# Activation slots and weight buffers at 2 KB boundaries of the on-chip memory

## Chip, cores and metric

The kernel runs on one core of a Trainium2 chip. The metric is device time in microseconds (us) of one execution; lower is better. The core has five engines with queues of their own: TensorE (PE in the profile; its weight loads are shown as PEld), VectorE (DVE), ScalarE (ACT), GpSimd (POOL) and SyncE (SP), which here issues the DMA transfers. Tiles lie in the on-chip memory (SBUF), which has 128 partitions; an address below is a byte offset within a partition and is the same in all 128.

## What is computed

Two small transformer-like blocks, one behind the other, on 256 tokens of width 1,024, all in 32-bit floats. Cut to the parts that make up the work:

```python
# first block, two layers
for l in range(DEPTH):
    h = rmsnorm(x, g_mix[l])
    # layer 0: conformer convolution of h @ w_in_a; layer 1: forgetting attention
    x = x + concat([mix, memory_attention(...)]) @ w_out[l]
    x = x + conv_ffn(rmsnorm(x, g_ffn[l]), w_up[l], w_dw_f[l], b_dw_f[l], w_down[l])
# second block: retention layer, a gated embedding, a sparse attention layer, a gated embedding
h = h + (silu(gate) * groupnorm(retention(q, k, v))) @ ret_w_out
h = h + sigmoid(rmsnorm(h) @ w_gate) * (p_i @ w_emb)
h = h + (silu(gate) * (g0 * o_compressed + g1 * o_selected + g2 * o_window)) @ nsa_w_out
```

Nearly all the arithmetic lies in products of a 1,024-wide or 2,816-wide activation with weights that are read once.

## The kernel before

Activations are kept transposed: a chunk is 128 features by 256 tokens, and a width of 1,024 makes eight chunks. Weights are one long stream of units, each 128 partitions by 1,024 floats (512 KB), in the order in which they are used.

To keep precision with the faster 32-bit matmul form, most operands are split in two, a rounded "hi" and a remainder "lo". One weight block times one chunk then is three matmuls (`mm3`, lines 543 to 546): hi by hi (544), hi by lo (545), lo by hi (546), where the first name is the weight block, which is loaded into the array (128 columns), and the second the activation half, which streams through it (256 columns). `proj` (line 557) walks the chunks of an activation, takes the next weight block with `wblk`, and calls `mm3`. In the first stage ("conv") unsplit weights are multiplied directly (line 562).

An activation chunk lies in a *slot*, a tile of 512 floats (2 KB per partition): its first KB is hi, its second lo. The class `Slots` (line 357) holds a list of free slots and hands out the one that has been free longest. 38 slots are allocated at line 399, and seven *late* ones in `phase("ffn0")` from a pool that opens there (line 433).

A weight unit arrives by a DMA of SyncE in a `raw` buffer (lines 476 and 477). ScalarE rounds it to `whi` (line 492), VectorE or GpSimd subtracts to give `wlo` (line 495), and TensorE reads eight blocks of 512 bytes per partition from each. There are four raw buffers (pool `wraw`) and six of each of the other two (pool `wspl`), 4 KB each. `LOOK` lets the splitting run some four units ahead of the multiplications.

Addresses: tiles are laid out in the order in which pools are opened and, within a pool, in the order in which tiles are allocated, each rounded up to 32 bytes. The pool `const` (line 392) comes first, then `wraw`, `wspl`, `fp`, `tiny`, and then the pools of the phases. The pool `const` begins at 16,512, behind a reserved area. In the kernel before, its first tiles are the 38 slots, then come `one`, `par`, `xall`, `cst`, `ones`, `mhalf`, `epsc`, `bgh` and the other small tiles, `onesT` (line 1089), `bgate` (line 1559) and `pcz0` last. By the layout of this kernel:

```
what                     first address   behind a 2 KB boundary (bytes)
slots 0 to 37            16512           128
par, xall                94368, 97920    160, 1664
raw, whi, wlo buffers    110400          1856   (4096 bytes each)
fp (working tiles)       175936          1856
late slots 38 to 44      198336          1728
```

The small tiles: `ones` holds ones for sums over partitions, `epsc` a constant added in a root, `onesT` the ones of a scan (line 1090 fills it), and `bg` the gates of the last attention (line 1560). The scheduler that builds the program does not keep the written order of independent instructions; it places them by a simulated time.

Of the kernel before, what the change touches and what calls it, by code (L numbers as in the profile page):

```python
# [18 lines left out]
F32 = mybir.dt.float32  # L19
# [5 lines left out]
P = 128  # L25
T = 256
# [361 lines left out]
def block_kernel(ctx, tc, A, out, WL, PL, CL, SL, stop=None, dbg=None):  # L388
# [3 lines left out]
    const = ctx.enter_context(tc.tile_pool(name="const", bufs=1))  # L392
# [3 lines left out]
    tiny = ctx.enter_context(tc.tile_pool(name="tiny", bufs=4))  # L396
    dram = ctx.enter_context(tc.tile_pool(name="dram", bufs=1, space=bass.MemoryType.DRAM))
    psum = ctx.enter_context(tc.tile_pool(name="psum", bufs=1, space=bass.MemoryType.PSUM))
    slots = Slots(const, NSLOTS - LATE)

    cnt = [0]
# [130 lines left out]
        return cst[:, o:o + n]  # L532

    ident = par[:, PL.off["ident"]:PL.off["ident"] + P]
    ones = const.tile([P, P], F32, name="ones")
    pool.memset(ones, 1.0)
    mhalf = const.tile([P, 2], F32, name="mhalf")
    pool.memset(mhalf, -0.5)
    epsc = const.tile([P, 2], F32, name="epsc")
    pool.memset(epsc, 1e-6)  # L540


# [532 lines left out]
    FR = 38  # L1075
# [10 lines left out]
    act.activation(za[0:FR, :], za[0:FR, :], AF.Exp, scale=-1.0)  # L1086
    act.activation(za[0:FR, :], za[0:FR, :], AF.Ln, bias=1.0)
    dve.scalar_tensor_tensor(zl[0:FR, :], z[0:FR, :], 0.0, za[0:FR, :], op0=OP.min, op1=OP.subtract)
    onesT = const.tile([FR, T], F32, name="onesT")
    pool.memset(onesT, 1.0)  # L1090
    cl = f1()
    dve.tensor_tensor_scan(cl[0:FR, :], onesT, zl[0:FR, :], 0.0, op0=OP.mult, op1=OP.add)
# [463 lines left out]
    pb = bank()  # L1556
    for tt in range(2):
        pe.transpose(pb[:, 64 * tt:64 * tt + 48], zb[0:48, P * tt:P * tt + P], ident[0:48, 0:48])
    bg = const.tile([P, 2, 48], F32, name="bgate")
    act.copy(bg, pb[:, 0:128].rearrange("p (t c) -> p t c", t=2)[:, :, 0:48])  # L1560

    SC128 = 128.0 ** -0.5
# [266 lines left out]
```

## Time and profile before

| | us |
|---|---|
| runs of the kernel before: lowest, median, highest | 1,216.21, 1,219.66, 1,224.07 |
| the profiled execution, whole | 1,224.89 |
| its span, first to last instruction | 1,223.1 |
| TensorE busy within the span | 1,177.8 |
| VectorE, ScalarE, GpSimd busy | 933.1, 720.3, 396.0 |

The mean granted TensorE clock of the profiled execution is 0.989. "Busy" of TensorE adds up the spans of pipelined matmul records that overlap, so it says when TensorE has work, not how fast it goes; the pace is read from start times. Lines are those of the kernel file, and a line of a helper such as `mm3` collects the work of all its callers. A tile is named without its buffer number, so the trace does not say which slot an instruction read; where the text does, it follows from the program's own list of instructions, which stand in the trace in the same order on TensorE.

### The profile page before, as it was taken

Reading aid. Unit: us, or ns where it says so; the run is one execution under the profiler, and the core shown is the slowest. Engines: PE = TensorE matmul, PEld = TensorE weight load, DVE = VectorE, ACT = ScalarE, POOL = GpSimd, SP = SyncE. Lnnn points to the kernel's source line nnn. Section 1 sums busy time; section 2 is a strip of 40 time slices with the busy share of each in tenths; the row PEclk is TensorE's granted clock in tenths of the full one; section 3 lists DMA queues with packets and bytes.
Section 4 is the critical chain, followed back from the end, with each engine's and each line's share of the span. In section 5 each row is a group of like instructions: output and inputs, shape, how many; then the busy total and the mean of one; then the engine's idle time right before and its main releaser. Section 6 shows DMA issues by size and latency. Waiting matters only on the chain.

```text
span 1223.1 us, 23147 instructions
## 1 busy us (share of the span) xinstructions
PE 1177.8 (96%) x8924; PEld 1128.9 (92%) x8924; DVE 933.1 (76%) x1610; ACT 720.3 (59%) x1336; POOL 396.0 (32%) x302
## 2 busy tenths in 40 slices
PE   7999999999999999899999999999999999999996
PEld 6888999999989999899999999999998899888996
DVE  1896799995568988998656876757896778979574
ACT  3855667665566766666554555445665756556545
POOL 3862412212413243222242222213444432222251
PEclk9999999999999999999999999999999999999998
DMA  9822545665544335555654655555566743332260
GB/s 352 294 96 66 172 159 190 204 206 184 182 137 138 122 129 173 174 188 193 203 183 155 199 169 176 189 169 184 163 199 233 249 139 104 121 104 96 87 207 35
DMA packets 59870, 205.60 MB, mean 168 GB/s; under 512 B 6640, under 2 KB 9072, under 8 KB 59760
## 3 DMA queue, kind: packets, MB, share of 16 engines
q1 hardware_dynamic: 59760, 204.12, 50.5%
q8 instruction: 70, 1.15, 0.4%
q14 instruction: 40, 0.33, 0.1%
HBM read 202.00 MB, written 2.10 MB: 167 GB/s over the span
## 4 chain that ended last, share of the span: by engine, by line
PE 79%; DVE 12%; ACT 4%; issue 3%; DMA 1%; POOL 0%; SPq 0%; DVEq 0%; ACTq 0%; POOLq 0%
PE acc L544 11%; PE acc L545 11%; PE acc L546 11%; PE s L544 5%; PE s L545 5%; PE s L546 5%; PE pt L544 4%; PE pt L545 4%; PE pt L546 4%; PE acc L562 4%; DVE wlo L495 3%; PE pt L562 2%; PE pt L665 2%; ACT whi L492 1%; DVE slot L595 1%
## 5 line engine op out<-in xcount | busy, mean ns | idle before, releaser
L492 ACT CAST whi<-raw 128x1024 fp32r<-128x1024 f32 x341 | 355.3, 1048 | 213.9 <-PE acc L545 90.1
L495 POOL TENSOR_TENSOR wlo<-raw,whi 128x1024 fp32r<-128x1024 f32 x94 | 231.7, 2465 | 535.5 <-ACT whi L492 428.3
L495 DVE TENSOR_TENSOR wlo<-raw,whi 128x1024 fp32r<-128x1024 f32 x247 | 322.8, 1309 | 102.9 <-ACT whi L492 99.6
L545 PE MATMUL acc<-slot,whi 128*128 128x256 f32 x1360 | 384.2, 283 | 0.5 <-DVE slot L595 0.2
L544 PE MATMUL acc<-slot,whi 128*128 128x256 f32 x1360 | 380.6, 283 | 4.0 <-ACT slot L592 1.8
L546 PE MATMUL acc<-slot,wlo 128*128 128x256 f32 x1360 | 382.7, 282 | 0.0
L544 PEld LDWEIGHTS acc<-slot,whi 128*128 128x128 f32 x1360 | 256.0, 189 | 6.1 <-ACT slot L592 2.0
L545 PEld LDWEIGHTS acc<-slot,whi 128*128 128x128 f32 x1360 | 257.8, 190 | 3.3 <-DVE slot L595 1.8
L546 PEld LDWEIGHTS acc<-slot,wlo 128*128 128x128 f32 x1360 | 257.8, 190 | 0.7
L544 PE MATMUL s<-slot,whi 128*128 128x256 f32 x508 | 144.1, 286 | 6.5 <-DVE ca L1009 4.0
L545 PE MATMUL s<-slot,whi 128*128 128x256 f32 x508 | 144.1, 284 | 1.5 <-DVE slot L581 1.5
L546 PE MATMUL s<-slot,wlo 128*128 128x256 f32 x508 | 143.2, 284 | 0.3 <-POOL wlo L495 0.3
L544 PE MATMUL pt<-slot,whi 128*128 128x256 f32 x468 | 131.3, 281 | 1.3 <-ACT slot L580 1.2
L545 PE MATMUL pt<-slot,whi 128*128 128x256 f32 x468 | 131.3, 281 | 0.0
L546 PE MATMUL pt<-slot,wlo 128*128 128x256 f32 x468 | 131.1, 280 | 0.0
L544 PEld LDWEIGHTS s<-slot,whi 128*128 128x128 f32 x508 | 96.7, 191 | 7.7 <-ACT whi L492 4.1
L545 PEld LDWEIGHTS s<-slot,whi 128*128 128x128 f32 x508 | 97.3, 192 | 1.7 <-DVE slot L581 1.7
L546 PEld LDWEIGHTS s<-slot,wlo 128*128 128x128 f32 x508 | 97.2, 192 | 0.5 <-POOL wlo L495 0.4
L610 POOL TENSOR_TENSOR sqa<-sqa,sq 128x256 f32<-128x256 f32 x54 | 56.2, 1044 | 118.4 <-ACT sq L614 117.4
L544 PEld LDWEIGHTS pt<-slot,whi 128*128 128x128 f32 x468 | 88.1, 188 | 1.8 <-ACT slot L580 1.4
L545 PEld LDWEIGHTS pt<-slot,whi 128*128 128x128 f32 x468 | 88.0, 188 | 0.0
L546 PEld LDWEIGHTS pt<-slot,wlo 128*128 128x128 f32 x468 | 87.9, 188 | 0.1
(381 smaller groups left out, 2102.3 us busy)
## 6 DMA issues: line engine op xcount, KB each, us to landing
raw<-ws SPq DMA_DIRECT2D x341, 512.0 KB, 3.5
wf<-ws SPq DMA_DIRECT2D x28, 512.0 KB, 8.2
xall<-xtok SPq DMA_DIRECT2D x2, 512.0 KB, 3.9
tok<-mtok SPq DMA_DIRECT2D x2, 512.0 KB, 10.2
mem<-memt SPq DMA_DIRECT2D x8, 128.0 KB, 6.1
emb<-em SPq DMA_DIRECT2D x4, 256.0 KB, 4.2
xall<-xt SPq DMA_DIRECT2D x4, 256.0 KB, 3.8
dm<-decay SPq DMA_DIRECT2D x4, 256.0 KB, 4.1
```

The lines of the kernel that those rows point to most:

```text
L492: act.copy(whi[i], raw[i])
L495: eng.tensor_tensor(wlo[i], raw[i], f32(whi[i]), op=OP.subtract)
L544: pe.matmul(ps, lhsT=ahi, rhs=bhi, start=start, stop=False)
L545: pe.matmul(ps, lhsT=ahi, rhs=blo, start=False, stop=False)
L546: pe.matmul(ps, lhsT=alo, rhs=bhi, start=False, stop=stop)
L562: pe.matmul(ps, lhsT=hi, rhs=s, start=start and k == 0, stop=stop and k == len(X) - 1)
L595: dve.scalar_tensor_tensor(s.lo, src, col, f32(s.hi), op0=OP.mult, op1=OP.subtract)
L610: pool.tensor_tensor(self.acc, self.acc, self.last, op=OP.add)
L665: pe.transpose(o, i, ident)
```

## The change

Three small tiles are allocated ahead of the slots, and one small tile is made wider. No operation is added, removed or moved in the text; `epsc` is filled in 56 columns where it was filled in two, and only its first column is read.

```diff
     psum = ctx.enter_context(tc.tile_pool(name="psum", bufs=1, space=bass.MemoryType.PSUM))
+
+    onesT = const.tile([38, T], F32, name="onesT")
+    ones = const.tile([P, P], F32, name="ones")
+    bg = const.tile([P, 2, 48], F32, name="bgate")
     slots = Slots(const, NSLOTS - LATE)
...
-    ones = const.tile([P, P], F32, name="ones")
     pool.memset(ones, 1.0)
...
-    epsc = const.tile([P, 2], F32, name="epsc")
+
+    epsc = const.tile([P, 56], F32, name="epsc")
     pool.memset(epsc, 1e-6)
...
-    onesT = const.tile([FR, T], F32, name="onesT")
     pool.memset(onesT, 1.0)
...
-    bg = const.tile([P, 2, 48], F32, name="bgate")
     act.copy(bg, pb[:, 0:128].rearrange("p (t c) -> p t c", t=2)[:, :, 0:48])
```

By the layout rule above, `onesT` (1,024 bytes), `ones` (512) and `bgate` (384) fill 16,512 to 18,432, which is 9 x 2,048. The slots begin there. The rest of the pool, with 216 bytes more for `epsc`, ends at 110,592, which is 54 x 2,048, and the raw, whi and wlo buffers begin there. Everything behind them moves by 192 bytes, so `fp` begins at 176,128 (0 behind a boundary), and the seven late slots at 198,528, which is 1,920 behind one.

## Rows read from the trace of the kernel before

**Rows 1.** The page: busy time (share of span), then the chain's shares by engine.
```profile
PE 1177.8 (96%) x8924; PEld 1128.9 (92%) x8924; DVE 933.1 (76%) x1610; ACT 720.3 (59%) x1336; POOL 396.0 (32%) x302
...
PE 79%; DVE 12%; ACT 4%; issue 3%; DMA 1%; POOL 0%; SPq 0%; DVEq 0%; ACTq 0%; POOLq 0%
```

**Rows 2.** Groups by line: busy us, mean ns of one, then idle before and releaser.
```profile
L545 PE MATMUL acc<-slot,whi 128*128 128x256 f32 x1360 | 384.2, 283 | 0.5 <-DVE slot L595 0.2
L546 PE MATMUL acc<-slot,wlo 128*128 128x256 f32 x1360 | 382.7, 282 | 0.0
L544 PE MATMUL acc<-slot,whi 128*128 128x256 f32 x1360 | 380.6, 283 | 4.0 <-ACT slot L592 1.8 <-DVE nq L1590 1.7 <-DVE slot L581 0.5
...
L544 PE MATMUL s<-slot,whi 128*128 128x256 f32 x508 | 144.1, 286 | 6.5 <-DVE ca L1009 4.0 <-ACT whi L492 2.6
...
L545 PE MATMUL pt<-slot,whi 128*128 128x256 f32 x468 | 131.3, 281 | 0.0
```

**Rows 3.** Timeline of TensorE, 1,506 intervals without a stall: start us, length us.
```profile
157.61 0.28 PE L546 MATMUL s<-slot,wlo 128*128 128x256 f32 x1
...
335.08 0.28 PE L546 MATMUL acc<-slot,wlo 128*128 128x256 f32 x1
```

**Rows 4.** The same view, another stretch, 50 intervals.
```profile
758.05 0.28 PE L545 MATMUL acc<-slot,whi 128*128 128x256 f32 x1
...
763.71 0.28 PE L544 MATMUL acc<-slot,whi 128*128 128x256 f32 x1
```

**Rows 5.** Windows: us, PE, PEld, DVE, ACT, POOL busy, clock, DMA share, GB/s.
```profile
157.60:335.10 177.50, 177.50 (x1509) 177.50 (x1508) 147.21 (x228) 111.09 (x182) 45.05 (x22) 1.00 0.58 188
...
646.40:806.10 159.70, 159.70 (x1141) 149.18 (x1140) 117.35 (x182) 81.52 (x119) 41.07 (x33) 1.00 0.53 174
```

**Rows 6.** Timeline of TensorE: the first and the last of 7,176 intervals between such matmuls.
```profile
95.99 0.28 PE L545 MATMUL acc<-slot,slot 128*128 128x256 f32 x1
...
1212.41 0.28 PE L546 MATMUL acc<-slot,wlo 128*128 128x256 f32 x1
```

**Rows 7.** Timeline of all engines, the first ten microseconds.
```profile
0.77 0.20 POOL L536 MEMSET ones<- 128x128 f32 x1
...
0.94 0.10 POOL L540 MEMSET epsc<- 128x2 f32 x1
...
5.58 0.30 POOL L1090 MEMSET onesT<- 38x256 f32 x1
...
6.19 0.56 POOL L688 TENSOR_TENSOR tn<-tn,mhalf 128x1 f32<-128x1 f32 x1
...
6.79 0.75 DVE L716 TENSOR_SCALAR xall<-xall,tn 128x1024 f32<-128x1024 f32 x1 [0.92 <-POOL tn L688]
...
7.60 0.69 PE L665 MATMUL acc<-par,xall 128*128 128x128 f32 x2 [7.60 <-DVE tn L687]
...
9.49 5.03 PE L562 MATMUL s<-sq,wf 128*128 128x256 f32 x11 [0.56 <-DMA wf<-ws]
```

**Rows 8.** Chain of waits at the start, in order of time: start us, us, what.
```profile
3.06 6.30 DMA wf<-ws
```

**Rows 9.** DMA issues: count, KB each, median us to landing.
```profile
raw<-ws SPq DMA_DIRECT2D x341, 512.0 KB, 3.5
...
xall<-xtok SPq DMA_DIRECT2D x2, 512.0 KB, 3.9
```

**Rows 10.** Timeline of TensorE: first and last of 702 matmuls that read late slots.
```profile
278.57 0.28 PE L544 MATMUL acc<-slot,whi 128*128 128x256 f32 x1
...
1178.25 0.28 PE L545 MATMUL acc<-slot,whi 128*128 128x256 f32 x1
```

**Rows 11.** The same view, slots by slots, 11 intervals.
```profile
351.28 0.28 PE L544 MATMUL s<-slot,slot 128*128 128x256 f32 x1
...
352.59 0.28 PE L546 MATMUL s<-slot,slot 128*128 128x256 f32 x1
```

**Rows 12.** Waits of TensorE, the longest: us in total, times, longest us.
```profile
PE acc L665 <- DVE tn L687: 7.6, 1, 7.6
```

## The prediction

> **What bounds the kernel now.** I read the page's busy shares and its chain of waits first. TensorE is busy 1,177.8 of 1,223.1 us, and 79% of the chain that ended last is its own work [rows 1]. No other engine comes near, so a change matters if it alters the pace at which matmuls follow each other, or adds a wait in front of them. The groups by line then say which matmuls: lines 544 to 546, the three products of one weight block with one activation chunk, stand 1,360, 508 and 468 times each, 3 x 2,336 = 7,008 matmuls [rows 2]. Their "mean ns of one" (281 to 286) is the length of a pipelined record, not the pace, so I took the pace from the timeline's start times. In a long stretch without a stall 1,506 intervals fill 335.08 - 157.61 = 177.47 us, 117.8 ns each [rows 3]. In another, 50 intervals fill 763.71 - 758.05 = 5.66 us, 113.2 ns each [rows 4]. Same shapes, same lines, and the granted clock is 1.00 around both [rows 5]: **there are two paces**. Sorting all 7,176 intervals between consecutive matmuls of this form (256 columns; first and last are in [rows 6]) into their 143 unbroken runs, 19 runs with 516 intervals keep the fast pace throughout, 113 runs with 6,354 intervals the slow one, 11 runs with 306 change on the way.
>
> The window from 157.6 to 335.1 us shows what else has room: TensorE busy for all 177.50 us, VectorE for 147.21, ScalarE for 111.09, DMA 58% [rows 5]. VectorE would have to grow by a fifth (177.5 / 147.2) to take over.
>
> **The change, part by part.** It removes and adds no instruction. Four allocations change, and with them addresses.
>
> *The padded epsc tile.* Its memset writes 56 columns where it wrote 2. A memset of 2 columns took 0.10 us, the one of 128 columns 0.20 [rows 7]; in between, 0.14, so GpSimd is 0.04 us later. Behind it GpSimd's in-order queue holds the other memsets and then the power of line 688 (6.19 us), for which VectorE's line 716 waits, and for that the first transposes at 7.60 us. TensorE's next matmul, at 9.49, waits for the first weights, which land 6.30 us behind their issue at 3.06 us [rows 8], and TensorE idles 0.56 us before it [rows 7]. That idle time hides the 0.04 us; without it 0.04 us would be the whole cost. I take 0.
>
> *Transfers.* Weights land in buffers that begin elsewhere. Only the first landing is on the path (6.30 us [rows 8]); later ones come while TensorE is busy throughout [rows 5]. Transfers of 512 KB to two differently placed tiles took 3.9 us (xall) and 3.5 us (raw) [rows 9], in other places of the queue, so this bounds an effect of placement to a tenth of 6.30 us, 0.6 us either way. I take 0.
>
> *VectorE, ScalarE, GpSimd.* The same operations on tiles in new places. By the 20% of room above their durations do not set the end; 0, and if VectorE did grow by a fifth, TensorE would start to wait.
>
> *TensorE's operands* are what is left. Before, slots 0 to 37 begin 128 bytes behind a 2 KB boundary, the seven late slots 1,728 behind, the weight buffers 1,856 behind. The three products read the slot's first, second and first KB, so line 545 alone crosses a 2 KB boundary in an early slot, and its records are no longer than those of 544 and 546 (283, 283, 282 ns) [rows 2]. Of the eight weight blocks (512 bytes each) of a buffer two cross one, and of the intervals of [rows 6] those of slots by weights average 117.4 to 117.6 ns for each of the eight places. So crossing a 2 KB boundary costs nothing here, and removing it gives nothing.
>
> But addresses do reach the pace. Early slots lie at 0 modulo 128 and weight buffers at 64, late slots at 64 like the weights. From the start times, 702 intervals behind a matmul that reads a late slot (first and last in [rows 10]) average 118.15 ns, those behind early slots with the same weights 117.41: 0.74 ns more where both operands have the same remainder. Where both are early slots (equal remainders again) a run of 11 takes 352.59 - 351.28 = 1.31 us, 119.1 ns each [rows 11], or 1.7 ns more. After the change early slots, late slots (1,920 behind a boundary) and weights all lie at 0 modulo 128: equal remainders everywhere. I take the row nearest to it, slots against weights: 0.74 ns x (7,008 - 702) = **+4.7 us**. The bounds: +1.7 ns x 6,306 = +10.7 us above; below, all slow runs at the fast pace, 6,354 x (117.8 - 113.2 = 4.6 ns) = -29.2 us, because no row shows an operand on a 2 KB boundary.
>
> [...]
>
> **The sum.** The profiled execution took 1,224.9 us (span 1,223.1 and 1.8 around it), 5.2 above the median 1,219.66 of the runs shown. It would become 1,229.6; the median 1,224.4. I predict 1,224 us.
>
> **The rivals.**
>
> *Fast pace.* Boundary-aligned operands could make runs settle at 113.2 ns. For it: both paces exist, and a run's pace is mostly fixed when it starts, so a small shift could decide it. Against it: among early slots and weights the remainders never vary, and yet both paces occur, so the address alone does not choose; and the equal remainders that the trace has are slower. Half of the slow intervals give -14.6 us (1,205), all give -29.2 (1,190). It passes 1% (12.2 us) from 2,650 of the 6,354 on.
> [...]
>
> *Slow pace.* Moving and weight reads now begin at the same place of a boundary, and a second step like that between the paces could come on top: 4.6 ns x 7,008 = +32 us (1,252), half of it 1,236. It decides from 1.74 ns per matmul on (12.2 us / 7,008). For it: the 119.1 ns of [rows 11] are nearly there. Against it: no run of more than five of the 143 averages over 119.6 ns.
>
> *Another order.* The scheduler places instructions by its own simulated times: line 1090's memset runs at 5.58 us, among the first [rows 7]. A longer memset and earlier tiles may move others, one TensorE wait more or less. TensorE's longest is 7.6 us [rows 12]; I allow 7.6 either way, 1,212 to 1,227, within 1%.
>
> *It does not do what it says.* Seven of 45 slots miss the boundary (1,920). At 4.6 ns their 702 intervals are worth 3 us; this changes no forecast.
>
> **How the numbers follow.** My forecast, a pace within about 1 ns of today's, gets 0.54 (its own range 1,215 to 1,232); the fast pace 0.24; the slow pace 0.14; another order 0.08. About 1% is what a measurement of this kernel can tell from no change. Faster by more: 0.23 of the fast case and 0.02 of the order, 0.25. Slower by more: 0.14, 0.02 of the forecast's tail and 0.02 of the order, 0.18. Within 1%: 0.57. The range 1,195 to 1,236 leaves out the lowest part of the fast case (0.07) and most of the slow one (0.12).
>
> **What the profile after would show.** Right: the same counts per line, runs that keep the slow pace at 118 to 119 ns, VectorE and ScalarE rows unchanged, the first weight matmul still at about 9.5 us. Wrong: unbroken runs near 113 ns in the long stretch of [rows 3] (fast), or above 120 (slow), or lines in another order with new waits in front of TensorE.

## The result and the profile after

The changed kernel took 1,229.79 us (median; 1,228.09 to 1,233.94), the kernel before beside it 1,221.63 us. The ratio is 1.0071, with a 95% interval from 1.0054 to 1.0088: 8 us slower, inside the 1% that the prediction called no change. The profiled execution took 1,233.94 us, its span 1,232.2 us against 1,223.1.

The page of the kernel after: busy times, the chain's shares, the groups of the three products (busy us, mean ns of one, idle before), one DMA row. The lines moved by four, so 548 to 550 are 544 to 546 of before.

```profile
PE 1188.6 (96%) x8924; PEld 1142.7 (93%) x8924; DVE 931.7 (76%) x1610; ACT 721.3 (59%) x1336; POOL 397.9 (32%) x302
...
PE 79%; DVE 12%; ACT 3%; issue 3%; DMA 1%; POOL 0%; SPq 0%; DVEq 0%; ACTq 0%; POOLq 0%
...
L549 PE MATMUL acc<-slot,whi 128*128 128x256 f32 x1360 | 386.8, 285 | 2.3 <-DVE slot L599 2.0
L548 PE MATMUL acc<-slot,whi 128*128 128x256 f32 x1360 | 383.7, 285 | 2.2 <-DVE nq L1592 1.6
L550 PE MATMUL acc<-slot,wlo 128*128 128x256 f32 x1360 | 385.8, 285 | 0.0
...
raw<-ws SPq DMA_DIRECT2D x341, 512.0 KB, 3.3
```

Counts are those of [rows 1], the chain too but for 1% of ScalarE; TensorE alone is busy longer, 1,188.6 us against 1,177.8, while VectorE, ScalarE and GpSimd stay within 2 us. The records grew from 283, 283 and 282 ns [rows 2] to 285. The order of TensorE's 8,924 matmuls is the same, which allows a comparison matmul by matmul.

The timeline of TensorE in the kernel after, first and last row of the stretch of [rows 3], again 1,506 intervals, and of the longest stretch but one, 1,123 intervals (start us, length us):

```profile
156.35 0.28 PE L550 MATMUL s<-slot,wlo 128*128 128x256 f32 x1
...
336.83 0.28 PE L550 MATMUL acc<-slot,wlo 128*128 128x256 f32 x1
...
517.76 0.28 PE L549 MATMUL pt<-slot,whi 128*128 128x256 f32 x1
...
652.11 0.28 PE L550 MATMUL acc<-slot,wlo 128*128 128x256 f32 x1
```

180.48 us / 1,506 = 119.8 ns each, against 117.8 before; 134.35 / 1,123 = 119.6 ns. The window of the long stretch (columns as in [rows 5]) shows that nothing else came up: TensorE is busy throughout, the clock is 1.00, VectorE needs 147.38 us where it needed 147.21.

```profile
156.40:336.80 180.40, 180.40 (x1507) 180.40 (x1507) 147.38 (x228) 110.97 (x182) 45.21 (x22) 1.00 0.55 185
```

Over all 7,188 intervals of this form (matmuls of 256 columns on operands split in hi and lo, in a stream without a stall) the mean is 119.56 ns, before 117.52. Of the 19 unbroken runs at the fast pace, one of which [rows 4] shows, a single one of nine intervals is left.

Between the same matmuls of the two traces, start to start, the 9.05 us of span (1,232.2 - 1,223.1) divide so:

```
intervals between 256-column matmuls of the split form      +14.6 us   (7,182 intervals, +2.03 ns each)
512-column matmuls that stream a weight buffer or a slot      -1.9 us   (493; those from weight buffers 233.5 -> 227.6 ns)
matmuls of the unsplit form                                  -0.4 us   (763)
everything else: pauses, slow clock, changes of shape        -3.4 us   (485)
ahead of the first and behind the last matmul                +0.2 us
```

The start is as forecast. The chain of the kernel after begins with the first weights' transfer, 6.03 us (before 6.30 [rows 8]), and the first weight matmul starts at 9.22 us (9.49 before [rows 7]).

```profile
3.06 6.03 DMA wf<-ws
```

### The profile page after: what moved, and what is told of

It is laid out like the page before. It is cut to its first block, busy times and chain, and to the rows that moved or that the text cites. A ratio compares the mean times of both kernels' runs of the same rounds, so it can differ in the third digit from the quotient of the medians.

```text
span 1232.2 us, 23147 instructions
## 1 busy us (share of the span) xinstructions
PE 1188.6 (96%) x8924; PEld 1142.7 (93%) x8924; DVE 931.7 (76%) x1610; ACT 721.3 (59%) x1336; POOL 397.9 (32%) x302
## 4 chain that ended last, share of the span: by engine, by line
PE 79%; DVE 12%; ACT 3%; issue 3%; DMA 1%; POOL 0%; SPq 0%; DVEq 0%; ACTq 0%; POOLq 0%
PE acc L549 12%; PE acc L548 12%; PE acc L550 12%; PE s L548 5%; PE s L549 5%; PE s L550 5%; PE pt L548 4%; PE pt L549 4%; PE pt L550 4%; PE acc L566 4%; DVE wlo L499 3%; PE pt L669 2%; PE pt L566 2%; DVE slot L599 1%; DVE slot L585 1%
## 5 line engine op out<-in xcount | busy, mean ns | idle before, releaser
L549 PEld LDWEIGHTS acc<-slot,whi 128*128 128x128 f32 x1360 | 260.9, 192 | 4.8 <-DVE slot L599 3.3
L548 PEld LDWEIGHTS acc<-slot,whi 128*128 128x128 f32 x1360 | 259.6, 192 | 4.2 <-DVE nq L1592 1.8
L550 PEld LDWEIGHTS acc<-slot,wlo 128*128 128x128 f32 x1360 | 260.6, 192 | 0.8
L548 PE MATMUL s<-slot,whi 128*128 128x256 f32 x508 | 146.0, 289 | 7.1 <-DVE ca L1013 3.7
L549 PE MATMUL s<-slot,whi 128*128 128x256 f32 x508 | 145.8, 288 | 1.1 <-DVE slot L585 1.1
L548 PE MATMUL pt<-slot,whi 128*128 128x256 f32 x468 | 132.7, 284 | 1.2 <-ACT slot L584 1.0
L549 PE MATMUL pt<-slot,whi 128*128 128x256 f32 x468 | 132.7, 284 | 0.0
L548 PEld LDWEIGHTS s<-slot,whi 128*128 128x128 f32 x508 | 98.7, 195 | 8.0 <-ACT whi L496 4.7
L549 PEld LDWEIGHTS s<-slot,whi 128*128 128x128 f32 x508 | 99.3, 196 | 1.4 <-DVE slot L585 1.3
L548 PEld LDWEIGHTS pt<-slot,whi 128*128 128x128 f32 x468 | 89.7, 192 | 1.7 <-ACT slot L584 1.2
L549 PEld LDWEIGHTS pt<-slot,whi 128*128 128x128 f32 x468 | 89.7, 192 | 0.0
```

Source lines behind the costliest of these rows:

```text
L548: pe.matmul(ps, lhsT=ahi, rhs=bhi, start=start, stop=False)
L549: pe.matmul(ps, lhsT=ahi, rhs=blo, start=False, stop=False)
L550: pe.matmul(ps, lhsT=alo, rhs=bhi, start=False, stop=stop)
```

## The experiments

The first theory after the result kept the prediction's unit: equal remainders modulo 128 slow a stream ("Theory A" below). It missed in the first three runs, and the map behind them gave the one that stands ("Theory D"): TensorE's pace depends on how far the weight operand begins behind the moving operand (in the map 120.0 ns at a distance of 0, 118.6 at 128, 117.8 at 192, 113.3 or 117.8 at 64), and the unit of 128 bytes is too small. Inside a slot and inside a weight buffer every operand begins a multiple of 256 bytes further (halves of 1 KB, blocks of 512 bytes), so modulo 256 each pair of tiles has one distance, "weights ahead of slots". Before: early slots 128 behind a boundary, weights 1,856, which is 64 modulo 256, distance 64 - 128 = 192 (modulo 256). After: 0. The rivals were that a 2 KB boundary itself costs, and that something other than addresses does. Times of each run stand beside runs of the kernel before on the same chip.

### One half of the change each, and a third place

The slots' half alone (the changed kernel with the narrow `epsc`, so weights lie 64 behind a multiple of 256; distance 64):

```diff
-    epsc = const.tile([P, 56], F32, name="epsc")
+    epsc = const.tile([P, 2], F32, name="epsc")
```

> The three small tiles stand ahead of the slots, but epsc keeps two columns: slots 0 to 37 begin on a 2 KB boundary, the weight buffers stay 1,856 bytes behind one (64 modulo 128), late slots 1,728 (64). Theory A (equal remainders modulo 128 of moving and weight operand slow the stream): the remainders differ again for the early slots, so the long stretch runs at 117.8 ns per matmul and the ratio to the kernel before is 0.998 to 1.003. Rival B (what slows is slots on a 2 KB boundary): 119.8 ns and a ratio of 1.007. Rival C (what slows is weight buffers on a boundary, whatever the slots): 117.8 ns and 1.000, as A.

Measured: 1,215.08 us, ratio 0.9935 [0.9922, 0.9947], mean interval 115.5 ns. The long stretch breaks up here; its best part, 822 intervals, in the timeline:

```profile
181.85 0.29 PE L550 MATMUL s<-slot,wlo 128*128 128x256 f32 x1
...
275.10 0.28 PE L550 MATMUL acc<-slot,wlo 128*128 128x256 f32 x1
```

93.25 us / 822 = 113.4 ns: half of the change makes the kernel faster, which none of the three theories had.

The weights' half alone (the kernel before with the wide `epsc`; slots at 128, weights on 2 KB boundaries, distance 128):

```diff
-    epsc = const.tile([P, 2], F32, name="epsc")
+    epsc = const.tile([P, 56], F32, name="epsc")
```

> The tiles stand as before and epsc has 56 columns: slots 0 to 37 stay 128 bytes behind a 2 KB boundary (0 modulo 128), weight buffers begin on one, late slots 1,920 behind. Theory A: equal remainders (0), so about 119.8 ns per matmul in the long stretch and a ratio of about 1.007. Rival B: slots off the boundary, 117.8 ns and 1.000. Rival C: 119.8 ns and 1.007, as A. In all three, matmuls that stream 512 columns out of a weight buffer take about 227.6 ns, as in the changed kernel, if that gain comes from the weight buffer's place alone.

Measured: 1,228.73 us, ratio 1.0046 [1.0032, 1.0060], mean 118.8 ns; the stretch of 1,506 intervals:

```profile
155.84 0.28 PE L546 MATMUL s<-slot,wlo 128*128 128x256 f32 x1
...
334.55 0.28 PE L546 MATMUL acc<-slot,wlo 128*128 128x256 f32 x1
```

178.71 / 1,506 = 118.7 ns, between what Rival B and what A and C expected. The 512-column matmuls out of a weight buffer took 232.4 ns and not 227.6, so that gain does not come from the weight buffer's place alone. So the halves do not add up: 0.9935 and 1.0046 alone, 1.0071 together. Slots and weights act as a pair.

The changed kernel with `epsc` of 72 columns, slots on 2 KB boundaries and weights 64 bytes further (distance 64, as in the slots' half alone, but reached through the weights):

> The changed kernel with epsc of 72 columns: slots on a 2 KB boundary, weight buffers 64 bytes behind one, late slots 1,984 behind (64 modulo 128). Theory A: early slots and weights differ modulo 128, so 117.8 ns in the long stretch and a ratio of 0.998 to 1.003. Rival B (slots on the boundary slow): 119.8 ns and 1.007. Rival C (weights on the boundary slow): 117.8 ns and 1.000.

Measured: 1,213.74 us, ratio 0.9917 [0.9904, 0.9931], mean 116.3 ns. 64 bytes of padding turn the slower kernel into a faster one, again outside all three expectations. How much of the time is at 113 ns differs from the slots' half alone at the same distance (there 2,338 intervals in runs under 114.7 ns, here 1,013), which the distance does not explain. Here the stretch of 1,506 stays whole; its first matmul, the first in it that reads a late slot, and its last:

```profile
155.79 0.28 PE L550 MATMUL s<-slot,wlo 128*128 128x256 f32 x1
...
276.75 0.28 PE L548 MATMUL acc<-slot,whi 128*128 128x256 f32 x1
...
332.24 0.28 PE L550 MATMUL acc<-slot,wlo 128*128 128x256 f32 x1
```

Up to the late slot 1,027 intervals took 117.8 ns each, the 479 behind it 115.8. So a stream in which late slots (distance 128) mix with early ones (64) can change its pace on the way.

### A map of the pace

A kernel that only streams: 96 matmuls in the pattern hi, lo, hi, with moving and weight tiles at chosen places.

> Not the kernel: a stream of matmuls alone, which leaves all of the reference's computation out. 48 pairs of places, moving operand 0, 64, 128, 192, 256 or 512 bytes behind a 2 KB boundary, weight blocks 0, 32, 64, 128, 192, 256, 320 or 384 behind one; each pair is 96 matmuls in the order of the three products, streamed twice, in opposite orders of the pairs. Theory A: pairs with equal remainders modulo 128 take about 2 ns more per matmul than those that differ by 64. Rival B: the rows with the moving operand at 0 are slow, whatever the weights. Rival C: the columns with weights at 0 (or at 0 modulo 128) are slow, whatever the moving operand. If the pace of a stream depends on how it started more than on the places, the two streams of one pair disagree, by up to 4.6 ns.

Its timeline, first and last of 96 matmuls with both operands at 0, then with weights 64 ahead:

```profile
456.22 0.39 PE L56 MATMUL ps<-mov,whi 128*128 128x256 f32 x1 [0.52 <-ACT o L59]
...
467.72 0.28 PE L58 MATMUL ps<-mov,wlo 128*128 128x256 f32 x1
468.52 0.39 PE L56 MATMUL ps<-mov,whi 128*128 128x256 f32 x1 [0.52 <-ACT o L59]
...
479.40 0.28 PE L58 MATMUL ps<-mov,wlo 128*128 128x256 f32 x1
```

11.50 us against 10.88 for 95 intervals. From the 13th matmul on a stream keeps one pace: 120.0 ns at distance 0 (the very first stream apart), 118.6 at 128 (one of 22 at 120.0), 117.8 in all 18 at 192, and at 64 now 113.3 (13 streams) and now 117.8 (9); only the distance modulo 256 mattered among places that are multiples of 64. So Theory A has the tendency right and the unit wrong, and Rivals B and C fall. In the long stretch the kernel before (192: 117.8), after (0: 119.8) and the weights' half (128: 118.7) stand where the map puts them. The short stretches at 113.2 ns of the kernel before [rows 4], at 192, have no like in it. The seven late slots fit only nearly (distance 128 before and after: 118.15 before [rows 10], about 119.3 after); they stand between early ones in the same streams. The map also has 512-column matmuls in which a weight buffer streams and the slot is the stationary operand, the one that is loaded: 226.6 ns once settled where both begin at the same place modulo 256, 233.1 where the stationary operand is 64 ahead. In the block the streamed weight buffer lay at 64 and the stationary slot 64 ahead of it before (233.5 ns), and both lie at 0 after (227.6): the -1.9 us above.

### Equal places away from any boundary

The kernel before with padding such that slots begin at 320 and weights at 64 behind a 2 KB boundary: distance 0, as in the changed kernel, but nothing on a boundary.

```diff
+    epsc = const.tile([P, 48], F32, name="epsc")
     slots = Slots(const, NSLOTS - LATE)
...
-    epsc = const.tile([P, 2], F32, name="epsc")
     pool.memset(epsc, 1e-6)
+    spacer = const.tile([P, 24], F32, name="spacer")
+    pool.memset(spacer, 0.0)
```

> The order of before, with 192 bytes (epsc) ahead of the slots and 96 more behind: early slots begin 320 bytes behind a 2 KB boundary and weight buffers 64 behind one, so neither lies on a boundary and both have the remainder 64 modulo 256. Theory D (the pace is set by the distance of the moving operand's start from the weight block's, modulo 256: 0 gives 120.0 ns, 64 gives 117.8, 128 gives 118.6, 192 gives 113.3 or 117.8): distance 0, so 119.5 to 120 ns per matmul in the long stretch and a ratio of 1.006 to 1.009, as in the changed kernel. Rival B (a place on the 2 KB boundary itself is what slows): 117.8 ns and 1.000.

Measured: 1,230.41 us, ratio 1.0061 [1.0042, 1.0080], mean 119.56 ns, equal to the changed kernel's to the second decimal. The long stretch:

```profile
157.15 0.28 PE L548 MATMUL s<-slot,wlo 128*128 128x256 f32 x1
...
337.63 0.28 PE L548 MATMUL acc<-slot,wlo 128*128 128x256 f32 x1
```

180.48 us, as in the changed kernel. This settles the cause: the 2 KB boundary has no part in it, equal places modulo 256 give the whole change of pace without it. In this run too 512-column matmuls from weight buffers took 227.7 ns, and pauses and unsplit matmuls gave back 3.3 us.

### The late slots too

The slots' half with 64 bytes of padding ahead of the late slots, so that all weights lie 64 ahead of all slots.

```diff
+    spacer = tiny.tile([P, 16], F32, tag="spacer", name="spacer", bufs=1)
+    pool.memset(spacer, 0.0)
```

> The kernel with slots on 2 KB boundaries and weight buffers 64 modulo 256, plus 64 bytes ahead of the late slots, which so come from 192 to 0 modulo 256. Theory D: the late slots' distance goes from 128 to 192 as well; their 700 intervals go from 119.4 to about 115 ns, some 3 us, and mixed runs can keep the fast pace: ratio 0.985 to 0.992, below the 0.9935 of the same kernel with late slots untouched. Rival (only the early slots' place matters, the late ones are too few): 0.9935, within its interval.

Measured: 1,207.08 us, ratio 0.9875 [0.9859, 0.9891], faster than both kernels; mean 114.6 ns, 5,220 of 7,181 intervals in runs under 114.7. The stretch of 1,123 intervals that took 134.35 us in the changed kernel:

```profile
508.54 0.28 PE L551 MATMUL pt<-slot,whi 128*128 128x256 f32 x1
...
635.84 0.28 PE L552 MATMUL acc<-slot,wlo 128*128 128x256 f32 x1
```

127.30 us, 113.4 ns each. Against the kernel before, matmul by matmul, the 256-column intervals shrank by 20.8 us and the pauses grew by 3.0.

### What chooses between two paces, and finer steps

A second map, moving tiles fixed at 0, weights in steps of 16 bytes and some between, five streams each in mixed order:

> A stream of matmuls alone, which leaves the reference's computation out. Moving operand 0 bytes behind a 2 KB boundary, weight blocks at every 16 bytes from 0 to 240 behind one, and at 40, 52, 56, 60, 68, 72, 76 and 88; 96 matmuls each, five times each in shuffled order. Theory D at a finer grain: one value for each distance modulo 256 (120.0 ns at 0, 118.6 at 128, 117.8 at 64 of distance, that is weights at 192), and two values, 113.3 and 117.8, at distance 192 (weights at 64). If which of the two is taken depends on how a stream starts, the five streams of that place disagree; if the first weights' place decides, they agree. A place at which all five take 113.3 ns would be better than any tried.

Measured: 113.3 ns in all five streams at distances 52, 76 and 88, three of five at 64; 117.8 at 56 and 192; 119 to 120 at 0, 40, 60, 112, 144 and 160; the rest in between, most of them at 116.7 to 118.7. Two streams at the same distance, 64, in the timeline, first three and last matmul of each:

```profile
611.61 0.39 PE L55 MATMUL ps<-mov,whi 128*128 128x256 f32 x1 [0.52 <-ACT o L58]
611.84 0.28 PE L56 MATMUL ps<-mov,whi 128*128 128x256 f32 x1
611.95 0.28 PE L57 MATMUL ps<-mov,wlo 128*128 128x256 f32 x1
...
622.50 0.28 PE L57 MATMUL ps<-mov,wlo 128*128 128x256 f32 x1
...
1035.37 0.39 PE L55 MATMUL ps<-mov,whi 128*128 128x256 f32 x1 [0.52 <-ACT o L58]
1035.60 0.28 PE L56 MATMUL ps<-mov,whi 128*128 128x256 f32 x1
1035.71 0.28 PE L57 MATMUL ps<-mov,wlo 128*128 128x256 f32 x1
...
1046.67 0.28 PE L57 MATMUL ps<-mov,wlo 128*128 128x256 f32 x1
```

10.89 us and 11.30 us for the same 95 intervals with the same addresses. The fourth matmul starts 0.47 us behind the first in one (at 612.08) and 0.46 us in the other (at 1035.83), and then each keeps its pace, 113.3 or 117.8. So at 64 the same addresses have both paces, and a stream keeps the one that it has from its 13th matmul on. This is the prediction's "a run's pace is mostly fixed when it starts", now with equal addresses.

### The distance 88 tried in the kernel, twice

First through the slots: they become views into one large tile, 40 bytes behind a multiple of 256, and weights lie 128 behind.

```diff
-        self.free += [pool.tile([P, 512], F32R, name=f"slot{i}") for i in range(self.n, self.n + n)]
+        big = pool.tile([P, 512 * n + 16], F32R, name=f"slots{self.n}")
+        self.free += [big[:, SHIFT + 512 * i:SHIFT + 512 * i + 512] for i in range(n)]
```

with `SHIFT = 10` (40 bytes), and as its control `SHIFT = 16` (64 bytes, distance 64):

> Slots are views into one large tile (its early and its late part), shifted by 40 bytes; all slots lie 40 behind a multiple of 256, all weight buffers 128, so every weight buffer lies 88 ahead of every slot modulo 256. Theory (the distance modulo 256 sets the pace, and at 88 the map had 113.3 ns in all five streams, at 64 only in three of five): nearly all 256-column streams at 113 to 114 ns, mean 113.3 to 113.7; against the 114.61 of all slots at distance 64, 7,300 intervals x about 1.1 ns = 8 us less, 1,199 us, ratio 0.978 to 0.984. Rival A (what chooses among the two paces is not the address but how a stream starts): about one interval in seven still at 118 ns, as at distance 64, 1,207 us, ratio 0.987. Rival B (the large tile makes the program wait more, since views of one tile are tracked together): pauses between streams grow; then this run is slower than at distance 64 in shifted views, with the same pace.

> The control for the run at distance 88: the same views into one large tile, shifted by 64 bytes in place of 40, so weights lie 64 ahead of all slots modulo 256; same order of instructions as at 88. Theory: as in the kernel with all slots at distance 64 and no views, 114.6 ns mean with one interval in seven at about 118, ratio 0.985 to 0.990, and 6 to 9 us above the run at 88. Rival A: the same time as at 88 within 2 us. Rival B: slower than 0.990 through pauses.

Measured: 1,234.84 us at 88, ratio 1.0085 [1.0070, 1.0100], the slowest kernel of all; 1,211.51 us for the control, 0.9895 [0.9876, 0.9915]. The stretch of 1,506 at 88, then the control's stretches of 1,506 and 1,150:

```profile
155.64 0.28 PE L552 MATMUL s<-slots,wlo 128*128 128x256 f32 x1
...
336.34 0.28 PE L552 MATMUL acc<-slots,wlo 128*128 128x256 f32 x1
```

```profile
156.52 0.28 PE L552 MATMUL s<-slots,wlo 128*128 128x256 f32 x1
...
333.89 0.28 PE L552 MATMUL acc<-slots,wlo 128*128 128x256 f32 x1
...
508.43 0.28 PE L551 MATMUL s<-slots,whi 128*128 128x256 f32 x1
...
638.79 0.28 PE L552 MATMUL acc<-slots,wlo 128*128 128x256 f32 x1
```

180.70 / 1,506 = 120.0 ns at 88; in the control 117.8 and, in another stretch at the same distance, 130.36 / 1,150 = 113.4 (mean of all 115.7, where 114.6 was expected). So neither theory nor rivals held at 88. The views are innocent, for the control has them. What the map had not varied is the place of the moving tile off multiples of 64; a third map did.

> A map of the pace alone (the block's computation is left out; the time says nothing of the kernel): streams of 96 matmuls of 256 columns, moving tiles at 0, 8, 16, 32, 40 or 56 modulo 256, weights 0, 52, 64, 76, 88 or 192 ahead of them, four streams of each pair in mixed order. Theory 1 (a moving operand that begins off a multiple of 64 bytes pays by itself, which is why slots at 40 with weights 88 ahead ran at 119.8 ns): row 0 repeats 120.0, 113.3, 113.3 or 117.8, 113.3, 113.3, 117.8 ns; rows 8, 16, 40 and 56 (and 32 if the step is 64) stand near 120 at all distances. Theory 2 (what counts is the place of the weights against 64: weights at 128 behind slots at 40 are a whole multiple, weights at 88 are not): pairs whose weights lie at a multiple of 64 differ from the others. Rival (distance alone decides, and the kernel with slots at 40 was slow for another reason, such as the operands' writers): all rows are alike.

Measured (settled pace in ns, four streams of each pair):

```
moving at   weights ahead by 0    52      64             76              88             192
 0           120.0              113.3   113.3 to 117.8  113.3 to 120.0  113.3          117.8
32           120.0              113.3   113.3 to 117.8  113.3           113.3          117.8
16           116.7 to 118.3     118.9   113.3           116.6 to 120.0  118.3 to 120.0 113.3 to 118.3
 8           120.0              120.0+  120.0+          120.5+          120.0          120.0
40           120.0              120.0+  120.0+          120.0+          117.8 to 120.0 120.0
56           121.1              120.7   120.9           120.0           120.9          120.0+
```

(+: some of the four up to 122.2, one 124.5.) Theory 1 held for 8, 40 and 56: these rows have no stream at 113.3 ns, whatever the distance. Rows 0 and 32 agree, so 64 is not the step. Row 16 goes against it: it lost the fast pace at 52 and 88 but has it in all four streams at 64 and in two at 192. The rival, distance alone, is out. Two streams, moving at 8 with weights 52 ahead and moving at 32 with weights 64 ahead:

```profile
32.07 0.39 PE L56 MATMUL ps<-mov,whi 128*128 128x256 f32 x1 [0.52 <-ACT o L59]
...
43.58 0.28 PE L58 MATMUL ps<-mov,wlo 128*128 128x256 f32 x1
...
277.24 0.38 PE L56 MATMUL ps<-mov,whi 128*128 128x256 f32 x1 [0.52 <-ACT o L59]
...
288.13 0.28 PE L58 MATMUL ps<-mov,wlo 128*128 128x256 f32 x1
```

11.51 us against 10.89 for 95 intervals.

Then through the weights: slots on multiples of 256, weight buffers as views shifted by 24 bytes, 88 behind. To make room there are ten weight buffers in place of twelve, and splitting runs one unit less ahead; the control has the same without the shift (`SHIFT = 0`).

```diff
-WBUFS = 6
-LOOK = 4 * UNIT + 768
+SHIFT = 6
+PITCH = UNIT + 64
+WBUFS = 5
+LOOK = 3 * UNIT + 768
...
-            whi[i] = wspl.tile([P, UNIT], F32R, tag="whi", name=f"whi{i}")
+            whi[i] = wspl.tile([P, PITCH], F32R, tag="whi", name=f"whi{i}")[:, SHIFT:SHIFT + UNIT]
```

(`wlo` and `wf` alike.)

> All slots, late ones too, begin on multiples of 256; the weight buffers (10 in place of 12, split one unit later, to make room) are views shifted by 24 bytes and begin 88 behind a multiple of 256. By the map, moving operands on a multiple of 32 with weights 88 ahead ran at 113.3 ns in all nine streams. Theory: mean of the 256-column streams 113.3 to 113.7 ns; against 114.6 at distance 64 some 7,200 x 1.1 = 8 us less; with what the two missing buffers cost (unknown, the control shows it) 8 us below the control; if they cost nothing 1,199 us, ratio 0.981. Rival: in the block a stream's start chooses its pace at 88 as at 64, one in seven near 118 ns, and this run equals its control.

> Control of the run before: the same ten weight buffers, not shifted, 64 behind a multiple of 256, all slots on multiples of 256. Theory: mean about 114.6 to 115.7 ns as in the two kernels with all weights 64 ahead; the time 1,207 us (ratio 0.9875) plus whatever two fewer buffers cost, and 6 to 10 us above the run with weights at 88. Rival: equal to the run at 88 within 2 us.

Measured: 1,204.78 us (1,204.39 to 1,204.87), ratio 0.9852 [0.9835, 0.9868], the fastest of all, though its interval overlaps that of the padded late slots; the control 1,209.97 us (1,209.53 to 1,211.61), 0.9898 [0.9883, 0.9913]. The difference of 5.2 us is near the expected one, but not from the expected place: the mean interval is 115.95 ns at 88 and 114.86 in the control. Two stretches of the run at 88, of 1,510 and 1,192 intervals, and its group of GpSimd's subtraction:

```profile
152.97 0.28 PE L553 MATMUL s<-slot,whi 128*128 128x256 f32 x1
...
334.17 0.28 PE L554 MATMUL acc<-slot,wlo 128*128 128x256 f32 x1
...
502.69 0.28 PE L554 MATMUL acc<-slot,wlo 128*128 128x256 f32 x1
...
637.79 0.28 PE L554 MATMUL acc<-slot,wlo 128*128 128x256 f32 x1
...
L501 POOL TENSOR_TENSOR wlo<-raw,whi 128x1024 fp32r<-128x1024 f32 x94 | 197.6, 2103 | 583.6 <-ACT whi L498 454.5
```

and the same group in its control:

```profile
L501 POOL TENSOR_TENSOR wlo<-raw,whi 128x1024 fp32r<-128x1024 f32 x94 | 235.5, 2507 | 560.9 <-ACT whi L498 411.2
```

The second stretch ran at 135.10 / 1,192 = 113.3 ns, the first at 181.20 / 1,510 = 120.0, at the same distance. So 88 also has two paces in the kernel, 113.3 and 120.0, and the one long stretch that settled at 120.0 cost 1,510 x 6.7 ns = 10 us. Start to start against the control, the 256-column intervals cost 7.8 us more and everything else but the 512-column ones 15 us less. GpSimd's 94 subtractions were 38 us shorter in sum, so that, as an estimate from the two means, each lo buffer was ready 0.4 us sooner behind its hi buffer; that this shortened the pauses was not tested apart from the pace.

Part of the 15 us is TensorE's clock. Ahead of 1,195 us five stretches of the control, 20.4 us in sum, have a granted clock of 0.50, each close to a wait of TensorE; at 88 there are two, 10.2 us. Two of the control's, in the columns of [rows 5]:

```profile
495.90:499.30 3.40, 3.40 (x17) 3.40 (x18) 3.40 (x3) 2.90 (x6) 2.77 (x1) 0.51 0.72 249
584.70:588.10 3.40, 3.40 (x18) 3.40 (x17) 2.51 (x3) 2.16 (x5) 0.00 (x0) 0.50 0.67 190
```

A 256-column interval takes 213 ns there, so by an estimate from these figures 10.2 us more of it cost 10.2 x (1 - 115 / 213) = 4.7 us. All four executions at 88 have a mean granted clock of 0.992 to 0.994, the control's 0.988 to 0.992. The slow clock marks starts of streams as well: the fast stretch at 88 begins at 502.69 us, where a stretch of slow clock ends; in the control the pace was 113.3 ns for 725 intervals up to a wait of 2.06 us at 581.9, and 117.8 for 445 behind the slow stretch that ends at 588.1.

## Why the prediction was right, and where a term was off

**What held.** *TensorE's pace is what a change of address can reach*: the 256-column intervals alone moved by +14.6 us, and the transfers, the memset and the other engines stayed where the sum had them. *The padded epsc*: the first weight matmul did not start later. *Transfers*: the first landing moved by 0.27 us, inside the 0.6 allowed. *The 2 KB boundary gives nothing*: the equal places of 320 and 64 cost as much as those on a boundary (1.0061 against 1.0071). *Equal places are slower*: the sign was right; of the two rows behind it only that of slots by slots shows the distance that the change makes. One sign of being right did not come: unbroken stretches were to keep 118 to 119 ns, and the long one ran at 119.8.

**The term that was off** is the pace: 0.74 ns per matmul, +4.7 us, taken from the late slots as the nearest row. Measured were +2.03 ns and +14.6 us, above the upper bound of +10.7 us that [rows 11] gave. The step that failed is "equal remainders modulo 128". Modulo 256 the late slots lay 128 from the weights, a third case (118.6 ns in the map), and only the slots by slots of [rows 11] were at distance 0; their 1.7 ns, called a bound, was the nearest row. Both remainders fitted the few distances that the trace of before shows (192, 128, 0), so the trace could not choose; the rows from different tiles at different distances should have been kept apart rather than pooled by the smaller modulus.

**Why the time came out near the forecast all the same.** That it did is luck in part. The profiled execution grew by 9.05 us against the 4.7 forecast, because three things that the sum held at nothing gave 5.7 us back: 512-column matmuls (-1.9, the other side of equal places, as the first map shows), unsplit ones (-0.4) and pauses (-3.4). (The sum also started from 1,219.66 us, the median of three runs before; that of six is 1,221.63.) Pauses moved against the pace in most runs, -5.2 us in the weights' half (intervals +9.3), +5.1 in the slots' half (-14.4), +3.0 with the late slots too (-20.8), though not with the weights moved to 64 (-1.7 with -8.7) or in the control through views (-0.3 with -13.3). What is called pauses here holds the stretches at a granted clock of 0.50 too, and their number differs from run to run: up to the last one near the end, 20.4 us before, 23.8 after, 13.6 with the weights moved to 64, 17.0 in the control through views. Without the intervals that lie in such a stretch in only one of the two traces, both exceptions come to +1.7 us, and the sign is against the pace in every run. A slower TensorE finds its inputs ready, a faster one waits for them: that reading fits these runs and was not tested by itself.

**The rivals.** *Fast pace* did not happen here; an address that brings it lies one padding away: weights 64 ahead of all slots give it for most of the kernel, worth 15 us, though no boundary is needed for it. The argument against it, that an address alone does not choose as both paces occur at one distance, is right as far as it goes (at 64 the map has 113.3 and 117.8 ns for the same addresses), but distance decides which paces there are, and at 0 it is nearly always the slow one (mean 119.56 ns; of the stretches at 113 ns one of nine intervals is left). *Slow pace* was the direction: its limit of 1.74 ns per matmul was passed (2.03), and the 1% was not, through what was given back. Its objection, that no run of more than five averages over 119.6 ns, told of the distances 192 and 128; at distance 0 the trace had only short runs such as [rows 11]. *Another order* did not come: TensorE's order is the same, and its longest wait, below, is that of [rows 12].

```profile
PE acc L669 <- DVE tn L691: 7.6, 1, 7.6
```

**Not settled.** What in the chip makes the distance count was not tested. Nor was what in the first intervals settles the pace of a stream, which leaves up to 10 us of the best kernel open. Why a moving operand at 16 keeps the fast pace at other distances than one at 0 stays open too.

## What to carry to other kernels

Where TensorE is busy throughout and the record of one matmul tells little (283 ns before, 285 after), take the pace from start times and sort it by the addresses of both operands; 64 bytes of padding between the pools were worth more here (1.0071 to 0.9917) than the change itself. Keep every distance between moving and weight tiles that occurs as a case of its own, and do not fold them by a remainder that the trace can't prove. And test the two halves of an alignment separately, since they can act as a pair (here 0.9935 and 1.0046 alone, 1.0071 together). Before the rest of a difference is put down to waiting, set the granted clock of both traces beside it (here an estimated 4.7 of 15 us).

## What the runs showed of the hardware that was not expected

- The pace of split 32-bit matmuls of 256 columns at a granted clock of 1.00 takes few values, 113.3, 117.8, 118.6 and 120.0 ns among them. Among places that are multiples of 64 the distance of weights and moving operand modulo 256 says which can occur (0: 120.0; 64: 113.3 or 117.8; 128: 118.6, in one of 22 streams 120.0; 192: 117.8, in short runs of the kernel before 113.2). Where one distance holds throughout, a stream keeps its pace from its first dozen matmuls on, in the kernel for up to 1,510 intervals; where two mix it can change (64 and 128: 117.8, then 115.8 ns).
- A moving operand that begins at 8, 40 or 56 bytes modulo 256 lost the fast pace: its streams ran at 117.8 to 124.5 ns, nearly all at 120 or more. At 32 it ran as at 0 (113.3 ns in all streams at distances 52 and 88), and at 16 it kept 113.3 ns at distance 64 and lost it at 52 (118.9) and 88 (118.3 to 120.0).
- 512-column matmuls that stream a weight buffer went the other way than the 256-column ones: 226.6 ns at distance 0, 233.1 with the stationary operand 64 ahead, where those had 120.0 and 113.3 or 117.8.
- GpSimd's subtraction of 128x1,024 took 2,507 ns with all weight buffers on multiples of 64 and 2,103 ns with the hi buffer that it reads and the lo buffer that it writes 24 bytes further (the raw buffer stayed). VectorE's subtraction of the same shape went from 1,307 to 1,287 ns.
- Stretches of 3.4 and 6.8 us at a granted clock of 0.50 lie close to waits of TensorE (of 1.6 to 3.0 us in the kernels before and after), and a 256-column interval takes 213 ns in them. The pace behind one need not be the pace ahead of it (113.3 ns, then 117.8).
